# Norms by two products with ones, an inverse root and a Newton step, in a two-layer encoder trunk on one core

## The chip, the cores and the metric

The kernel runs on one core of a Trainium2 chip. The time is device microseconds of one execution, the median over runs. The engines are PE (TensorE, with its weight loads PEld), DVE (VectorE), ACT (ScalarE), POOL (GpSimd) and SP (SyncE, which only issues DMAs here). Each engine works through its own queue in order.

## The reference, cut to what matters

`x` is 512 x 1024. Layer 0 has an mLSTM token mixer, layer 1 a band attention over keys and values that both come from the output of layer 0; each layer ends in a gated MLP, the channel mixer. What the change touches is the RMSNorm ahead of three of these blocks:

```python
def rmsnorm(x, g):
    x32 = x.astype(jnp.float32)
    y = x32 * lax.rsqrt(jnp.mean(x32 * x32, axis=-1, keepdims=True) + EPS)
    return (y * g.astype(jnp.float32)).astype(x.dtype)

# layer 0: x = x + concat(mLSTM, memory attention) @ w_out
x = x + conv_ffn(rmsnorm(x, norm_ffn_g[0]), ...)          # place 1
k, v = split(rmsnorm(x, kv_norm_g) @ w_kv)                # place 2
# layer 1: h = rmsnorm(x, norm_mix_g[1]), the same factor as place 2
x = x + concat(band attention, memory attention) @ w_out
x = x + conv_ffn(rmsnorm(x, norm_ffn_g[1]), ...)          # place 3
```

The fourth norm (ahead of layer 0) and the last one are done by other code and stay.

## The kernel before

Activations are kept transposed: `xT[j]` is a tile of 128 features by 512 tokens, eight tiles for the 1024 features. Every matrix product is done in three passes over a high and a low part (`mm3`, lines 158 to 160: high x high, high x low, low x high), each a 128x512 matmul. High parts are casts on ACT (line 114), low parts subtractions on DVE (line 115). A *unit* is one such group of three; a projection `project` of 1024 features onto 128 columns has eight units, and a weight tile goes through a raw buffer (`wr`, loaded by SP at line 127), a high and a low one (`wh`, `wl`), three of each. A cast into `wh` therefore waits for the last product that reads the buffer three projections back.

For three tiles of each channel mixer (`up` of tiles 1, 2 and 3) the low part is made without DVE: `summed_weights` casts the high part on ACT (line 147), writes its negative on ACT into a `pt` buffer (line 148), and POOL issues a DMA that reads the weights once more and adds them there (line 149).

A norm's factor depends on the token, so it is a row of 512 values that is wanted on all 128 partitions. The class `Norm` does this. While the tiles of `x` are finished, `add` sums their squares into `acc` (a tile of 128 x 512, a buffer of the tag `rb`), and `scaled` makes the high and low parts of the tiles times the gain, without the factor; the products run on these, and their results are multiplied by `row` afterwards. `finish` turns `acc` into `row`. It is a generator woven into the units of the projections that follow: `yield 5.4` lets 5 units of the filler be issued, and the rest is carried on to the next yield. In the three places the filler is: the first `gate` and `up` projections of channel mixer 0 (place 1) and of channel mixer 1 (place 3), 16 units; and the first value and key projections of layer 1 (place 2). A `row` used by `plain` multiplies the products of `gate` (line 670), by `forms` the tiles of `x` (line 685), and by `project_pair` the values and keys (line 1293), where PE then transposes the values (line 1304).

The same row by two products with ones, an inverse root on ACT and a Newton step on DVE stands already in the mLSTM heads (lines 1197 to 1202), for another norm.

In the three places the framework's scheduler sets the order of the work that the program issues, and then each engine keeps it.

Of the kernel before, what the change touches and what calls it, by code (L numbers as in the profile page):

```python
# [9 lines left out]
F32 = mybir.dt.float32  # L10
F32R = mybir.dt.float32r
I32 = mybir.dt.int32
AF = mybir.ActivationFunctionType
ALU = mybir.AluOpType
AX = mybir.AxisListType

P = 128
D = 1024
S = 512
KT = D // P  # L20
TT = S // P
# [9 lines left out]
EPS = 1e-6  # L31
# [16 lines left out]
def f(ap):  # L48
    return ap.bitcast(F32)
# [3 lines left out]
def trunk(  # L53
# [18 lines left out]
    nc = tc.nc  # L72
    V, A, G = nc.vector, nc.scalar, nc.gpsimd

    cpool = ctx.enter_context(tc.tile_pool(name="cpool", bufs=1))
# [8 lines left out]
    def sb(tag, shape, dtype=F32):  # L84
        count[0] += 1
        return pool.tile(shape, dtype, tag=tag, name=f"{tag}{count[0]}", bufs=bufs[tag])

    def ps(tag):
        count[0] += 1
        return psum.tile([P, S], F32, tag=tag, name=f"p{tag}{count[0]}", bufs=pbufs[tag])  # L90

    def small(n=4):
# [5 lines left out]
    ones = cpool.tile([P, P], F32, name="ones")  # L98
    V.memset(ones, 1.0)
    onesr = cpool.tile([P, P], F32R, name="onesr")  # L100
# [5 lines left out]
        out=maskf, in_=maskf, pattern=[[1, P]], base=0, channel_multiplier=-1,  # L106
        compare_op=ALU.is_ge, fill=NEG,
    )
    HEADS = (slice(0, HD), slice(HD, P))

    pin = tc.keep_in_program_order
# [125 lines left out]
    class Norm:  # L237
# [14 lines left out]
        def finish(self):  # L252

            yield 5.4
            o = ps("sc")
            for T in range(TT):
                tc.keep_in_program_order(
                    nc.tensor.matmul(
                        o[:, T : T + 1], self.acc[:, T * P : (T + 1) * P], ones[:, 0:1], start=True, stop=True
                    )  # L260
                )
            self.factor(o[:, :TT])
            yield 8.4
            self.spread()

        def factor(self, o):
            self.scale(o)
            self.diagonals()

        def scale(self, o):  # L270
            v = small()
# [133 lines left out]
    with tc.manual_schedule(engines={mybir.EngineType.PE, mybir.EngineType.Activation, mybir.EngineType.DVE}):  # L405
# [9 lines left out]
        for q in range(KT // 2 + 1):  # L415
            if q < KT // 2:
# [6 lines left out]
                hi, lo = sb("u", [P, S], F32R), sb("u", [P, S], F32R)  # L423
# [50 lines left out]
    def head_queries(t, scale=1.0):  # L474
        qs, ls = ([sb("u", [P, S], F32R) for _ in range(2)] for _ in range(2))
        for h, r in enumerate(HEADS):
            G.memset(f(ls[h])[HEADS[1 - h], :], 0.0)
            A.activation(qs[h][r, :], t[r, :], AF.Copy, scale=scale)
            V.scalar_tensor_tensor(ls[h][r, :], t[r, :], scale, f(qs[h])[r, :], op0=ALU.mult, op1=ALU.subtract)
        for h, r in enumerate(HEADS):  # L480
            A.copy(qs[h][HEADS[1 - h], :], f(qs[h])[r, :])
        return qs, ls

    def head_keys(t):
        ks = [sb("u", [P, S], F32R) for _ in range(2)]
        for h, r in enumerate(HEADS):
            A.copy(ks[h][r, :], t[r, :])
            V.tensor_tensor(out=ks[h][HEADS[1 - h], :], in0=t[r, :], in1=f(ks[h])[r, :], op=ALU.subtract)
        return ks
# [774 lines left out]
    for j in range(KT):  # L1264
        wh, wl = weights(rows(ffn_w_down[0], j * P, P, FT - LAST, FT), LAST, P)
        o = ps("mm")
# [252 lines left out]
```

## Time and profile before

| | |
|---|---|
| median of 3 runs | 1203.21 us (1202.51 to 1204.61) |
| profiled execution | 1202.59 us, its span 1200.6 us |
| granted PE clock | 0.998 |
| busy: PE, PEld, DVE, ACT, POOL | 99%, 87%, 78%, 60%, 12% of the span |
| norm at place 1, 2, 3: column sums on PE | at 278.4, 627.4, 843.6 us |

Times in the profile count from the start of the span. A row of a timeline gives start, duration (both us), engine, line, operation, tile written and tiles read (buffer numbers left out), shapes, count, and in brackets the idle time of that engine just before and what ended it. `SPq` and `POOLq` rows are issues of DMAs. A PE row's duration is modelled and overlaps with the next one; the distance from row to row is what a matmul costs.

### The profile page before, as it was taken

What the parts mean: (1) busy time and instruction counts of PE and PEld (TensorE: products, weight loads), DVE (VectorE), ACT (ScalarE), POOL (GpSimd) and SP (SyncE); (2) the same over time, 40 slices, a digit from 0 to 9 for tenths busy, and PEclk for the clock granted to TensorE, in tenths of its full rate; (3) what the DMA queues carried; (4) which work ended last, traced back from release to release, by engine and by line L of the source; (5) the groups of instructions that cost most, each with busy time, mean ns of one, the idle gap of its engine ahead of it and who ended that gap; (6) DMA issues with size and microseconds to landing.
All of it is one profiled execution on the core that took longest, in us unless ns stands there. A gap on an engine that the chain in (4) does not pass through costs nothing.

```text
span 1200.6 us, 18610 instructions
## 1 busy us (share of the span) xinstructions
PE 1182.9 (99%) x6963; PEld 1046.7 (87%) x6963; DVE 940.4 (78%) x1670; ACT 723.3 (60%) x1270; POOL 146.9 (12%) x234
## 2 busy tenths in 40 slices
PE   9999999999999999999999999999999999999997
PEld 8988888878899999999888888888789999999986
DVE  6877797787968777777698888997896877777755
ACT  4547797655656555555566677775565655555545
POOL 0203201011021111111020000101101011011100
PEclk9999999999999999999999999999999999999999
DMA  8636422448466677665563313244836465666551
GB/s 278 202 106 155 102 73 71 145 137 190 102 139 171 157 163 163 158 145 117 142 212 112 88 59 96 73 139 152 185 86 143 120 142 135 141 141 138 118 158 70
DMA packets 208747, 162.83 MB, mean 136 GB/s; under 512 B 8484, under 2 KB 188170, under 8 KB 208658
## 3 DMA queue, kind: packets, MB, share of 16 engines
q1 hardware_dynamic: 186450, 120.78, 34.5%
q0 software_dynamic: 22208, 40.87, 18.1%
q8 instruction: 54, 0.88, 0.3%
q14 instruction: 35, 0.29, 0.1%
HBM read 133.09 MB, written 32.47 MB: 138 GB/s over the span
## 4 chain that ended last, share of the span: by engine, by line
PE 78%; issue 12%; DVE 3%; DMA 3%; ACT 2%; POOL 1%; SPq 0%; POOLq 0%; ACTq 0%; DVEq 0%
PE pmm L158 15%; PE pmm L159 15%; PE pmm L160 15%; PE ptr L159 5%; PE ptr L158 5%; PE ptr L160 5%; PE psc L160 5%; PE psc L159 5%; PE psc L158 5%; DMA pt<-in_ffn_w_up_dram 2%; PE psc L497 1%; PE ptr L1346 1%; POOL xspill L611 1%; PE ptr L1367 0%; PE ptr L1368 0%
## 5 line engine op out<-in xcount | busy, mean ns | idle before, releaser
L158 PE MATMUL pmm<-u,wh 128*128 128x512 f32 (+1 forms) x968 | 335.6, 347 | 2.2 <-ACT u L114 2.1
L159 PE MATMUL pmm<-u,wh 128*128 128x512 f32 (+1 forms) x968 | 333.4, 345 | 0.0
L160 PE MATMUL pmm<-u,wl 128*128 128x512 f32 (+1 forms) x968 | 333.2, 345 | 0.0
L115 DVE TENSOR_TENSOR wl<-wr,wh 128x1024 fp32r<-128x1024 f32 (+4 forms) x172 | 195.2, 1136 | 110.0 <-ACT wh L114 108.9
L114 ACT CAST wh<-wr 128x1024 fp32r<-128x1024 f32 (+4 forms) x172 | 168.6, 981 | 98.0 <-PE pmm L159 43.1
L158 PEld LDWEIGHTS pmm<-u,wh 128*128 128x128 f32 x968 | 183.6, 190 | 21.1 <-ACT u L114 3.1
L160 PEld LDWEIGHTS pmm<-u,wl 128*128 128x128 f32 x968 | 183.6, 190 | 20.9
L159 PEld LDWEIGHTS pmm<-u,wh 128*128 128x128 f32 x968 | 183.8, 190 | 18.6 <-DVE u L115 0.6
L159 PE MATMUL ptr<-u,wh 128*128 128x512 f32 x272 | 106.5, 392 | 0.0
L158 PE MATMUL ptr<-u,wh 128*128 128x512 f32 x272 | 106.4, 392 | 0.0
L160 PE MATMUL ptr<-u,wl 128*128 128x512 f32 x272 | 105.8, 389 | 0.0
L733 POOL DMA_DIRECT2D xspill<-t x64 | 56.1, 877 | 401.0 <-ACT t L732 391.4
L160 PE MATMUL pmm<-u,u 128*128 128x256 f32 x296 | 84.0, 284 | 0.2 <-DVE u L115 0.2
L158 PE MATMUL pmm<-u,u 128*128 128x256 f32 x296 | 84.0, 284 | 0.0
L159 PE MATMUL pmm<-u,u 128*128 128x256 f32 x296 | 83.8, 283 | 0.0
L158 PE MATMUL psc<-u,wh 128*128 128x256 f32 (+1 forms) x232 | 76.1, 328 | 0.0
L159 PE MATMUL psc<-u,wh 128*128 128x256 f32 (+1 forms) x232 | 75.9, 327 | 0.0
L732 ACT COPY t<-ptr 128x512 f32<-128x512 f32 x64 | 37.4, 585 | 62.2 <-PE ptr L160 62.2
L115 DVE TENSOR_TENSOR u<-pt,u 128x512 fp32r<-128x512 f32 x102 | 69.8, 688 | 6.2 <-ACT u L114 3.0
L114 ACT CAST u<-pt 128x512 fp32r<-128x512 f32 x102 | 63.0, 617 | 11.4 <-DVE pt L848 11.3
L911 ACT ACTIVATE t<-t 128x512 f32<-128x512 f32 x34 | 21.6, 634 | 79.4 <-DVE t L637 79.4
L115 DVE TENSOR_TENSOR u<-t,u 128x512 fp32r<-128x512 f32 x78 | 53.4, 688 | 20.3 <-ACT u L114 19.8
(281 smaller groups left out, 2559.2 us busy)
## 6 DMA issues: line engine op xcount, KB each, us to landing
wr<-in_ffn_w_up_dram SPq DMA_DIRECT2D x54, 512.0 KB, 4.8
pt<-in_ffn_w_up_dram SPq DMA_DIRECT2D x34, 512.0 KB, 6.5
wr<-in_ffn_w_down_dram SPq DMA_DIRECT2D x34, 512.0 KB, 3.8
xspill<-t POOLq DMA_DIRECT2D x64, 256.0 KB, 4.8
wr<-in_a_w_in_dram SPq DMA_DIRECT2D x20, 512.0 KB, 3.9
xspill<-u POOLq DMA_DIRECT2D x32, 256.0 KB, 2.9
u<-xspill SPq DMA_DIRECT2D x32, 256.0 KB, 5.1
wr<-in_w_kv_dram SPq DMA_DIRECT2D x12, 512.0 KB, 4.1
```

The lines of the kernel that those rows point to most:

```text
L114: high = A.copy(hi, src) if on_act else V.tensor_copy(hi, src)
L115: low = V.tensor_tensor(out=lo, in0=src, in1=f(hi), op=ALU.subtract)
L158: nc.tensor.matmul(o, lh, rh, start=first, stop=False, skip_group_check=more)
L159: nc.tensor.matmul(o, lh, rl, start=False, stop=False, skip_group_check=more)
L160: nc.tensor.matmul(o, ll, rh, start=False, stop=last, skip_group_check=more)
L497: nc.tensor.matmul(o, a, b, start=first and i == 0, stop=i == 1)
L611: pin(G.dma_start(xspill[j], xT[j]))
L732: A.copy(t, o)
L733: G.dma_start(xspill[j], t, accum_op=ALU.add)
L911: A.activation(self.acc, self.acc, AF.Silu)
L1346: nc.tensor.transpose(tp[:, b * P : (b + 1) * P], es[T, h][:, b * P : (b + 1) * P], ident)
```

## The change

`finish` is rewritten and `factor` goes. Before: after 5 units, four matmuls with one column of ones sum `acc` over the partitions for 128 tokens each (tokens on partitions); then on DVE a shift-and-multiply start and three Newton steps on 128 x 4 values, a split into high and low, and two diagonal matrices of 128 x 512; after 13 units two products with ones spread these over all partitions, and a copy makes `row`. Now: after 5 units `acc` plus a constant is split into `hi` (ACT) and `lo` (DVE); after 8 units two products with ones sum and spread in one; ACT takes the inverse root, and DVE does one Newton step on 128 x 512. The constant is `epsc`, a new 128 x 1 tile.

```diff
+    epsc = cpool.tile([P, 1], F32, name="epsc")
+    V.memset(epsc, EPS * D / P)
...
         def finish(self):
 
             yield 5.4
+            hi, lo = sb("t", [P, S], F32R), sb("t", [P, S], F32R)
+            A.activation(hi, self.acc, AF.Identity, bias=epsc)
+            V.scalar_tensor_tensor(lo, self.acc, epsc, f(hi), op0=ALU.add, op1=ALU.subtract)
+            yield 2.6
             o = ps("sc")
-            for T in range(TT):
-                tc.keep_in_program_order(
-                    nc.tensor.matmul(
-                        o[:, T : T + 1], self.acc[:, T * P : (T + 1) * P], ones[:, 0:1], start=True, stop=True
-                    )
-                )
-            self.factor(o[:, :TT])
-            yield 8.4
-            self.spread()
-
-        def factor(self, o):
-            self.scale(o)
-            self.diagonals()
+            for i, part in enumerate((hi, lo)):
+                nc.tensor.matmul(o, onesr, part, start=i == 0, stop=i == 1)
+            self.row, t = sb("rb", [P, S]), sb("t", [P, S])
+            A.activation(self.row, o, AF.Abs_reciprocal_sqrt, scale=1.0 / D)
+            V.tensor_mul(t, self.row, self.row)
+            V.scalar_tensor_tensor(t, t, -0.5 / D, o, op0=ALU.mult, op1=ALU.mult)
+            V.scalar_tensor_tensor(self.row, t, 1.5, self.row, op0=ALU.add, op1=ALU.mult)
```

The lines below the new tile are three further down in the changed kernel, and those below `finish` one further (line 148 is 151 there, line 644 is 645).

PE's queue at place 1 before, from the fifth unit of `gate` (`pmm`) on; the column sums stand between the fifth and the sixth:

```order
L158 MATMUL pmm_2884<-u_2753,wh_2880 128x512
L159 MATMUL pmm_2884<-u_2754,wh_2880 128x512
L160 MATMUL pmm_2884<-u_2753,wl_2881 128x512
L258 MATMUL psc_2900<-ones,rb_2715 128x1 x4
L158 MATMUL pmm_2884<-u_2793,wh_2880 128x512
```

And in the changed kernel, from the eighth unit of `gate` to the first of `up` (`psc_2930`):

```order
L161 MATMUL pmm_2886<-u_2875,wh_2882 128x512
L162 MATMUL pmm_2886<-u_2876,wh_2882 128x512
L163 MATMUL pmm_2886<-u_2875,wl_2883 128x512
L264 MATMUL psc_2915<-t_2902,onesr 128x512
L264 MATMUL psc_2915<-t_2903,onesr 128x512
L161 MATMUL psc_2930<-u_2719,wh_2926 128x512
```

The column sums are gone, and the pair with ones, which stood after the fifth unit of `up`, now stands between `gate` and `up`.

ACT's queue at place 3 before, from the last tile of `x` (squares and gain) on:

```order
L249 ACTIVATE t_9053<-u_8449 128x512
L286 ACTIVATE u_9056<-u_8449,cols_519 128x512
L147 CAST wh_9224<-wr_9222 128x1024
L148 ACTIVATE pt_9064<-wh_9224 128x1024
L644 ACTIVATE t_9160<-t_9161,cols_771 128x512
```

And in the changed kernel:

```order
L252 ACTIVATE t_9015<-u_8411 128x512
L287 ACTIVATE u_9018<-u_8411,cols_521 128x512
L259 ACTIVATE t_9049<-rb_8860,epsc 128x512
L150 CAST wh_9166<-wr_9164 128x1024
L266 ACT_TABLE_LOAD
L266 ACTIVATE rb_9065<-psc_9062 128x512
L151 ACTIVATE pt_9026<-wh_9166 128x1024
L645 ACTIVATE t_9102<-t_9103,cols_773 128x512
```

`hi` (L259) stands ahead of the cast of the high part of `up`, tile 1; a table load and the inverse root (L266) stand between that cast and the write of its negative (L151). At place 1 the order is the same without the table load; at place 2 there is a load too, and a plain weight cast stands ahead of it. Over the whole program ACT has two table loads more.

## The prediction

> **What bounds the kernel now.** I read the page first, then the waits of the matmul engine (PE), then the timelines of all engines around the three norms, and last the shares of the DMA queues there. The page's engine table, and the second longest wait of PE (engine, line, what it waited for: total us, times, longest; the longest, 2.1 us, stands ahead of the first norm):
>
> ```profile
> PE 1182.9 (99%) x6963; PEld 1046.7 (87%) x6963; DVE 940.4 (78%) x1670; ACT 723.3 (60%) x1270; POOL 146.9 (12%) x234
> PE psc L160 <- DMA pt<-in_ffn_w_up_dram: 1.7, 2, 1.1
> ```
>
> PE is busy all the time and hardly waits, so PE time removed is time won, unless PE then waits longer. That one is the only wait near the norms: the third product of project `up` of tile 1 needs the low weight part that POOL accumulates by DMA (L149). Place 1 is the first mixer's norm, place 2 the norm ahead of token mixer B, place 3 the second mixer's norm. PE at place 1 (start, us, line, operation, and idle time before it in brackets):
>
> ```profile
> 270.02 0.39 PE L160 MATMUL pmm<-u,wl 128*128 128x512 f32 x1
> ...
> 278.18 0.39 PE L160 MATMUL pmm<-u,wl 128*128 128x512 f32 x1
> 278.41 0.95 PE L258 MATMUL psc<-ones,rb 128*128 128x1 f32 x8
> ...
> 281.39 0.39 PE L158 MATMUL psc<-u,wh 128*128 128x512 f32 x1
> ...
> 293.99 0.50 PE L160 MATMUL psc<-u,pt 128*128 128x512 f32 x1 [0.61 <-DMA pt<-in_ffn_w_up_dram]
> ```
>
> **The change, part by part.** *The column sums (L258) go.* Between the first two rows lie 36 steps: (278.18 - 270.02)/36 = 0.227 us each. From the L258 row to the 281.39 row lie nine products, 9 x 0.227 = 2.04 us, but 2.98 passed: the four small matmuls cost 0.94 us. The same at the other two places, nine products after the L258 row:
>
> ```profile
> 627.40 0.95 PE L258 MATMUL psc<-ones,rb 128*128 128x1 f32 x8
> 630.39 0.39 PE L158 MATMUL pmm<-u,wh 128*128 128x512 f32 x1
> 843.62 0.95 PE L258 MATMUL psc<-ones,rb 128*128 128x1 f32 x8
> 846.61 0.39 PE L158 MATMUL psc<-u,wh 128*128 128x512 f32 x1
> ```
>
> 2.99 - 2.04 = 0.95 at both. I take 0.94 three times: 2.82 us off PE. The pair of products with ones (L234) has the same shapes as before and is only moved, from after 13 units to after 8; zero.
>
> *Inputs of the pair.* It now needs `hi` (ACT) and `lo` (DVE) of the sum of squares. DVE at place 1:
>
> ```profile
> 277.25 0.69 DVE L250 TENSOR_TENSOR rb<-rb,t 128x512 f32<-128x512 f32 x1
> 277.85 0.75 DVE L287 SCALAR_TENSOR_TENSOR u<-u,cols,u 128x512 fp32r<-128x512 f32 x1
> 279.39 0.16 DVE L272 TENSOR_SCALAR s<-psc 128x4 f32<-128x4 f32 x1 [0.79 <-PE psc L258]
> 282.06 1.29 DVE L221 TENSOR_TENSOR t<-ident,s 128x512 fp32r<-128x512 f32 x2
> 285.46 0.69 DVE L282 COPY rb<-psc 128x512 f32<-128x512 f32 x1 [2.12 <-PE psc L234]
> 290.76 1.22 DVE L115 TENSOR_TENSOR wl<-wr,wh 128x1024 fp32r<-128x1024 f32 x1
> ```
>
> The sum is ready at 277.94. ACT is idle then (its next row is 281.40, below): `hi` by about 278.75, at the 0.6 to 0.8 us of ACT's 128x512 operations. `lo`, like L287, 0.75 us behind it, by 279.4. PE reaches the pair at 278.41 + 9 x 0.227 = 280.45. Cover 1.0 us, so no wait; if it were gone, each 0.1 us of it would cost PE 0.1. DVE loses the run 279.39 to 283.35 and the copy, 4.6 us, and gets `lo` and three Newton steps, 0.75 + 3 x 0.69 = 2.8; DVE does not bound, zero.
>
> *ACT and the DMA behind it.* This decides. ACT gets `hi`, the inverse root, and at places 2 and 3 one more table load, 3 x 1.3 + 2 x 1.3 = 6.5 us of an engine that is 60% busy. But it is an ordered queue, and the inverse root now stands between L147 and L148, whose result POOL's accumulating DMA waits for, and `up` of tile 1 behind that. ACT, SP and POOL at places 1 and 3, and PE's wait at place 3:
>
> ```profile
> 281.40 1.05 ACT L147 CAST wh<-wr 128x1024 fp32r<-128x1024 f32 x1 [4.18 <-issue]
> 282.49 1.06 ACT L148 ACTIVATE pt<-wh 128x1024 fp32r<-128x1024 f32 x1
> 283.85 1.62 POOL L149 DMA_DIRECT2D pt<-in_ffn_w_up_dram  x1 [7.12 <-ACT pt L148]
> 292.01 0.37 SPq L127 DMA_DIRECT2D wr<-in_ffn_w_up_dram  x1
> 846.62 1.05 ACT L147 CAST wh<-wr 128x1024 fp32r<-128x1024 f32 x1 [4.18 <-issue]
> 847.70 0.37 SPq L127 DMA_DIRECT2D wr<-in_ffn_w_up_dram  x1
> 847.70 1.06 ACT L148 ACTIVATE pt<-wh 128x1024 fp32r<-128x1024 f32 x1
> 848.12 1.67 SPq L743 DMA_DIRECT2D pt<-in_ffn_w_up_dram  x2
> 849.06 1.63 POOL L149 DMA_DIRECT2D pt<-in_ffn_w_up_dram  x1 [7.12 <-ACT pt L148]
> 859.69 0.50 PE L160 MATMUL psc<-u,pt 128*128 128x512 f32 x1 [1.10 <-DMA pt<-in_ffn_w_up_dram]
> ```
>
> L147 starts as gate 0's products end (281.39 above) and free its buffer, so it moves 0.94 us forward with PE. The price of the inverse root and its load is that of the same formula in the mLSTM heads:
>
> ```profile
> 129.23 0.62 ACT L114 CAST t<-t 128x512 fp32r<-128x512 f32 x1 [2.48 <-DVE t L1189]
> 129.87 1.28 ACT L1199 ACT_TABLE_LOAD   x1
> 129.91 0.50 PE L1197 MATMUL psc<-t,onesr 128*128 128x512 f32 x1 [0.24 <-ACT t L114]
> 131.17 0.60 ACT L1199 ACTIVATE t<-psc 128x512 f32<-128x512 f32 x1
> ```
>
> The load starts where the cast ends and does not wait for PE. So at place 1 (no load): L147 at 280.46, root at 281.54, L148 at 282.14 instead of 282.49, POOL's issue 0.35 us earlier at 283.50. At place 3: L147 at 845.68, load 846.76, root 848.06, L148 848.66 instead of 847.70; POOL's issue 0.96 us later, at 850.02, while PE comes 0.94 us earlier. Does the landing follow that issue? The queue shares at place 3 (q1 is SP's queue, q0 POOL's: packets, MB, share of 16 engines), for the microseconds from 853, from 854 and from 858:
>
> ```profile
> q1 hardware_dynamic: 499, 0.26, 95.6%
> ...
> q0 software_dynamic: 208, 0.11, 86.4%
> q1 hardware_dynamic: 268, 0.13, 46.5%
> ...
> q1 hardware_dynamic: 218, 0.11, 40.4%
> q0 software_dynamic: 32, 0.02, 15.8%
> ```
>
> POOL issued at 849.06, yet in 853 it has no row, so it moves nothing, and in 854 it starts, as SP's three transfers (3 x 0.5 MB, issued 847.70 to 849.79) run out. So the landing hangs on SP's transfers, which wait for L147 and come 0.94 us earlier with PE. I take that for the sum: both waits, 0.61 and 1.10, stay, and the whole 0.94 is won at each place. What hides POOL's later issue is SP's 1.5 MB: the issue ends at 850.02 + 1.63 = 851.65, the earliest moment of those packets moves to 854.0 - 0.94 = 853.1, cover 1.4 us; beyond it each us costs one. The other end of the price, the landing following the issue, is 0.59 us at place 1 and 1.90 at place 3; the packets are nearer to the first.
>
> [...]
>
> *Place 2.* `row` is needed by the transposes of the values:
>
> ```profile
> 630.40 1.05 ACT L114 CAST wh<-wr 128x1024 fp32r<-128x1024 f32 x1 [3.57 <-issue]
> 635.17 0.69 DVE L1293 TENSOR_TENSOR t<-pmm,rb 128x512 f32<-128x512 f32 x1
> 636.32 0.60 PE L1304 MATMUL pmm<-ident,t 128*128 128x128 f32 x4
> ```
>
> The cast also follows PE (the wh buffer that the finished projection frees) and comes at 629.46; load and root end at 629.46 + 1.08 + 1.30 + 0.60 = 632.44; three DVE steps of 0.72 give `row` at 634.6, L1293 ends at 635.3; PE wants it at 636.32 - 0.94 = 635.38. Cover 0.1 us. This chains six steps whose rows are each good to some 0.05 us, so 0 to 0.3 us may be lost; I take zero.
>
> *What comes late next.* At place 1 `row` is ready 2 us earlier than before (root ends 282.14, plus 2.2: 284.3, instead of 286.15), so the split at 290.76 and SP's next load behind it (292.01) come up to 2 us earlier, 1.1 more than PE, and meet the tail of POOL's accumulation. The price lies between 0 and 0.5 us: at place 3, where SP's load already meets that tail (859.69 waits while 858 shows both queues), the wait is 1.10 against 0.61 at place 1. I take 0.2.
>
> Sum: 3 x 0.94 - 0.2 = 2.6 us. The profiled execution took 1202.59 (span 1200.6); the median of the runs is 1203.21, so 1200.6 by the median, 1200.0 by the profiled one. No change can be told within 0.2%, 2.4 us: 1200.8 to 1205.6.
>
> **The rivals.** *The landing follows POOL's issue.* Place 1 then wins 0.35, place 2 0.94, and place 3 loses 0.96: 0.33 us won, 1202.9. For it: the accumulation is on the path at both places. Against it: the packets above.
>
> *Slower: SP's next load overtakes the accumulation's tail.* It moves 0.52 MB, 2.0 us at the 0.26 MB a us of the row. If the tail stood still for that, each mixer would lose 2.0 us against 0.94 won; place 2 still wins 0.94: 2 x 2.0 - 2.82 = 1.2 us slower, 1204.4. It decides where that load starts ahead of POOL's last packet and the loss in each mixer is beyond 1.41 us. For it: in 858 the tail is down to 32 packets a us while SP's load starts. Against it: both still move there, and only at place 1 does the load come nearer.
>
> *Row late at place 2.* Cover is 0.1 us there, and all beyond it is PE idle. If the switch of tables held the root back by once more a load, 1.28 us, 1.2 us would be lost: 1201.8. For it: the cover is thin. Against it: the root followed its load at once in the mLSTM rows (1.30 us from start to start, 1.28 of it the load). [...]
>
> *The waits go too.* If the accumulation lost its queueing behind the 1.5 MB, up to 0.61 + 1.10 more would be won: 1198.9. No row speaks for it.
>
> **How the numbers follow.** The forecast (2.82 less 0 to 0.8: 1200.4 to 1201.2) has 0.62, the landing by issue 0.16, the overtaken tail 0.09, the late row 0.06, the waits gone 0.07. The range leaves out the two outer cases, 0.16 together, and takes in 1202.9 and 1200.4 with 0.5 to 1 us for the scatter of the runs (1202.51 to 1204.61 before): 1199.3 to 1203.4. Faster by over 0.2% (below 1200.8): 0.7 of the forecast, 0.43, and the last case, 0.07, 0.50. Slower by over 0.2% (above 1205.6) is beyond every case, 0.04 for what I do not see. The rest, 0.46, is no change.
>
> **What would show it.** PE's rows at the pair: no L258, no idle, steps of 0.227. POOL's issue at place 3 about 1 us later against L147, and PE's wait for `pt` still near 0.6 and 1.1; if that wait is near 3 us, the landing follows the issue. At place 2 no idle before the transposes. Wrong would be: a wait for `hi`, or waits for `pt` at tiles 2 and 3.

## The result and the profile after

The changed kernel takes 1198.72 us, the median of six runs (1198.22 to 1199.65), against 1203.20 for the kernel before beside it (1202.51 to 1204.61): ratio 0.9963, 95% interval 0.9950 to 0.9976. That is 4.5 us faster, and 0.6 us below the predicted range. Its profiled execution took 1198.67 us, span 1196.9 us, against 1202.59 and 1200.6 before.

The engine table of the page after:

```profile
PE 1181.6 (99%) x6939; PEld 1046.2 (87%) x6939; DVE 935.5 (78%) x1632; ACT 729.1 (61%) x1278; POOL 145.5 (12%) x234
```

24 PE rows are gone, eight for each norm, as predicted. Of the waits of PE over the whole program, the three longest after, the start's load, and the same load before:

```profile
PE pmm L161 <- ACT u L117: 2.1, 1, 2.1
PE psc L1198 <- ACT t L117: 1.5, 4, 0.4
PE pmm L161 <- ACT wh L117: 1.4, 1, 1.4
...
PE psc L421 <- DMA u<-in_mem_dram: 0.5, 1, 0.5
```

```profile
PE psc L420 <- DMA u<-in_mem_dram: 1.1, 1, 1.1
```

The line for `pt`, 1.7 us over two waits before, has no counterpart. PE at place 1, from the fifth unit of `gate` to the first product that reads `pt`:

```profile
279.29 0.39 PE L163 MATMUL pmm<-u,wl 128*128 128x512 f32 x1
...
281.57 0.62 PE L264 MATMUL psc<-t,onesr 128*128 128x512 f32 x2
282.03 0.40 PE L161 MATMUL psc<-u,wh 128*128 128x512 f32 x1
...
293.16 0.39 PE L162 MATMUL psc<-u,wh 128*128 128x512 f32 x1
293.48 0.50 PE L163 MATMUL psc<-u,pt 128*128 128x512 f32 x1
```

And at places 2 and 3, again from the fifth unit on:

```profile
626.66 0.39 PE L163 MATMUL pmm<-u,wl 128*128 128x512 f32 x1
...
628.93 0.63 PE L264 MATMUL psc<-t,onesr 128*128 128x512 f32 x2
...
634.86 0.66 PE L1305 MATMUL pmm<-ident,t 128*128 128x128 f32 x4
...
841.97 0.39 PE L163 MATMUL pmm<-u,wl 128*128 128x512 f32 x1
...
844.25 0.63 PE L264 MATMUL psc<-t,onesr 128*128 128x512 f32 x2
...
855.84 0.39 PE L162 MATMUL psc<-u,wh 128*128 128x512 f32 x1
856.06 0.39 PE L163 MATMUL psc<-u,pt 128*128 128x512 f32 x1
```

Before, the fifth units ended with these rows at places 2 and 3, and these rows stood just ahead of the product that waited at places 1 and 3 (293.99 and 859.69):

```profile
627.17 0.39 PE L160 MATMUL pmm<-u,wl 128*128 128x512 f32 x1
...
843.40 0.39 PE L160 MATMUL pmm<-u,wl 128*128 128x512 f32 x1
```

```profile
292.99 0.39 PE L159 MATMUL psc<-u,wh 128*128 128x512 f32 x1
...
858.20 0.39 PE L159 MATMUL psc<-u,wh 128*128 128x512 f32 x1
```

From the fifth unit to the same later row, before less after:

- place 1: (293.99 - 278.18) - (293.48 - 279.29) = 15.81 - 14.19 = 1.62 us;
- place 2: (636.32 - 627.17) - (634.86 - 626.66) = 9.15 - 8.20 = 0.95 us;
- place 3: (859.69 - 843.40) - (856.06 - 841.97) = 16.29 - 14.09 = 2.20 us.

The column sums are 0.94 of each. The rest, 0.7 and 1.3, is the wait for `pt`. Counted from row to row, less a step of 0.227, the product came 0.77 us late before and 0.09 after at place 1 (1.00 and 0.32 from the row ahead), and 1.26 before and 0 after at place 3 (1.49 and 0.22). The idle time in the brackets, 0.61 and 1.10, is 0.16 less, since a row's modelled 0.39 us reach beyond the step. The three places make 4.8 us, and the medians 4.5. The spans of the profiled pair differ by 3.7 only, because the profiled execution after has a loss at 250 us that the one before has not, far from the norms. There PE stands 2.11 us behind ACT in both kernels; the rows of 250 to 260 us, before and then after (after the span come busy us of PE, PEld, DVE, ACT and POOL, the granted PE clock, DMA share, GB/s):

```profile
250.00:260.00 10.00, 8.54 (x36) 6.78 (x37) 7.20 (x11) 5.40 (x10) 1.63 (x3) 1.00 0.51 166
```

```profile
250.00:260.00 10.00, 8.70 (x31) 7.11 (x32) 6.08 (x9) 4.14 (x9) 1.63 (x3) 0.83 0.42 136
```

The clock was granted at 0.83 and PE got through five products fewer, 5 x 0.227 = 1.1 us. The start, where the load's wait is 0.6 shorter, gives part of it back. A second profile of the changed kernel (after_again, below) has no wait for `pt` either, and the same 0.83 behind the hole.

ACT, SP and POOL at place 3 after:

```profile
844.25 1.05 ACT L150 CAST wh<-wr 128x1024 fp32r<-128x1024 f32 x1 [1.76 <-PE pmm L162]
845.32 1.28 ACT L266 ACT_TABLE_LOAD   x1
845.75 1.61 SPq L744 DMA_DIRECT2D pt<-in_ffn_w_up_dram  x2
846.61 0.60 ACT L266 ACTIVATE rb<-psc 128x512 f32<-128x512 f32 x1
847.11 1.05 ACT L151 ACTIVATE pt<-wh 128x1024 fp32r<-128x1024 f32 x1
848.46 1.63 POOL L152 DMA_DIRECT2D pt<-in_ffn_w_up_dram  x1 [7.94 <-ACT pt L151]
```

POOL's issue comes 4.21 us behind the cast of `wh` (2.44 before), nearly as late as the 4.34 of the prediction. And still no wait. So a late issue by itself does not make the wait. The shares of the DMA queues hold a third queue, q8, whose kind the page gives as instruction. In both pages it has 54 packets, one about every 22 us, and from one of them to the next PE and PEld together have 253 rows on average before and 254 after (181 to 314), so I read its packets as fetches of PE's instructions:

```profile
q8 instruction: 54, 0.88, 0.3%
```

The quarter microseconds in which such a packet starts near the accumulation (before from 291.50 and from 856.75; after from 295.00 and from 857.75):

```profile
q0 software_dynamic: 85, 0.04, 138.1%
q8 instruction: 1, 0.02, 23.7%
...
q0 software_dynamic: 89, 0.05, 143.6%
q8 instruction: 1, 0.02, 23.5%
```

```profile
q1 hardware_dynamic: 48, 0.05, 88.5%
q8 instruction: 1, 0.02, 23.0%
...
q1 hardware_dynamic: 165, 0.08, 111.7%
q8 instruction: 1, 0.02, 25.7%
```

One packet of 16 KB takes 23.7% of 16 engines over 0.25 us, 0.95 us of engine time, where the 85 packets beside it take 138.1%, 0.065 us each. That one of the sixteen is away for nearly 1 us is my estimate from these two numbers; no trace names the engine of a packet. Before, the packet falls into the accumulation both times (q0's row beside it), and in its last part; after, only SP's queue is beside it, the accumulation having landed. What POOL's queue moves at its end, place 3, before in half microseconds from 857.5:

```profile
q0 software_dynamic: 29, 0.01, 26.2%
...
q0 software_dynamic: 21, 0.01, 22.7%
...
q0 software_dynamic: 11, 0.01, 9.0%
```

and after from 854.5:

```profile
q0 software_dynamic: 128, 0.06, 98.1%
...
q0 software_dynamic: 13, 0.00, 7.9%
```

After, the queue goes from 128 packets to none within 1 us; before, it drips for 1.5 us behind the fetch, a few packets at a time.

### The profile page after: what moved, and what is told of

The parts are those of the page before. It is cut to its first block, busy times and chain, and to the rows that moved or that the text cites. A ratio compares the mean times of both kernels' runs of the same rounds, so it can differ in the third digit from the quotient of the medians.

```text
span 1196.9 us, 18533 instructions
## 1 busy us (share of the span) xinstructions
PE 1181.6 (99%) x6939; PEld 1046.2 (87%) x6939; DVE 935.5 (78%) x1632; ACT 729.1 (61%) x1278; POOL 145.5 (12%) x234
## 4 chain that ended last, share of the span: by engine, by line
PE 94%; DVE 3%; ACT 2%; issue 0%; DMA 0%; SPq 0%; ACTq 0%; DVEq 0%
PE pmm L161 18%; PE pmm L163 18%; PE pmm L162 18%; PE ptr L161 6%; PE ptr L162 6%; PE ptr L163 6%; PE psc L163 5%; PE psc L162 5%; PE psc L161 5%; PE psc L498 2%; PE ptr L1347 1%; PE ptr L581 1%; PE ptr L1368 1%; PE ptr L1369 1%; PE ptr L567 1%; ACT wh L117 0%
```

## The experiments

Two theories. *Fetch*: an instruction fetch of PE that falls into the accumulation makes it land late; the change takes 24 matmul rows of PE away, with their weight loads, so the fetches fall elsewhere. *Order*: in the kernel before, POOL's issue stands amid SP's issues, and after it behind them, and that lets the accumulation land earlier. In the table below C is the start of the cast of `wh` that precedes the write of the negative; the third to fifth columns belong to place 1, the others to place 3. All are us, the fetch to within 0.25, and the wait is PE's idle time for `pt` as the trace has it. A kernel ran beside one of five sets of runs of the kernel before, each set on one chip, so its median is to be set against that one: 1203.20 for after; 1202.07 for sums_kept, before_late2, before_few_warm and after_filled; 1202.90 for after_late2, after_late3, few_warm_late2 and after_more_warm; 1202.83 for after_again, after_filled_again, place2_only and places13; 1202.92 for the rest.

| kernel | median | POOL - C | fetch - C | wait | POOL - C | fetch - C | wait |
|---|---|---|---|---|---|---|---|
| before | 1203.20 | 2.45 | 10.1 | 0.61 | 2.44 | 10.1 | 1.10 |
| after | 1198.72 | 2.80 | 13.4 | 0 | 4.21 | 13.5 | 0 |
| after_again | 1198.32 | 2.79 | 12.8 | 0 | 4.21 | 13.2 | 0 |
| sums_kept | 1203.10 | 2.79 | 10.3 | 0.63 | 4.21 | 7.8 | 0.37 |
| before_late2 | 1201.77 | 4.63 | 10.2 | 0.57 | 4.64 | 7.4 | 0.67 |
| before_few_warm | 1202.74 | 2.45 | 13.6 | 0.23 | 2.45 | 14.9 | 0.64 |
| few_warm_again | | 2.45 | 13.7 | 0 | 2.44 | 13.4 | 0.20 |
| few_warm_late2 | 1203.26 | 4.63 | 13.9 | 0.26 | 4.63 | 13.8 | 0 |
| few_warm_late2_again | | 4.63 | 14.1 | 0 | 4.62 | 13.8 | 0 |
| after_filled | 1197.79 | 2.80 | 9.9 | 0.57 | 4.2 | 14 | 0 |
| after_filled_again | 1198.37 | 2.8 | 10.3 | 0.58 | 4.2 | 14.3 | 0 |
| after_more_warm | 1202.91 | 2.8 | 9.8 | 0.31 | 4.2 | 10.8 | 0 |
| place2_only | 1202.11 | 2.45 | 9.8 | 0.22 | 2.44 | 10.6 | 1.09 |
| places13 | 1199.35 | 2.8 | 13.0 | 0 | 4.2 | 14.8 | 0 |
| after_late2 | 1199.81 | 4.98 | 12.7 | 0 | 6.39 | 15.8 | 1.06 |
| after_late3 | 1202.72 | 6.63 | 15.2 | 1.16 | 8.04 | 16.9 | 2.52 |
| pair_later | 1198.77 | 2.45 | 13.9 | 0 | 2.44 | 12.9 | 0 |
| pair_later_again | | 2.45 | 14.6 | 0.19 | 2.45 | 13.2 | 0.18 |

**The column sums back in.** The changed kernel with the four matmuls kept, their result unused:

```diff
+            for T in range(TT):
+                tc.keep_in_program_order(
+                    nc.tensor.matmul(
+                        o[:, T : T + 1], self.acc[:, T * P : (T + 1) * P], ones[:, 0:1], start=True, stop=True
+                    )
+                )
             yield 2.6
```

> The changed kernel with the four column-sum matmuls put back after the fifth unit of each norm, their result unused. Only PE's queue gets longer again, by 0.94 us and 16 PE instructions at each place; ACT, POOL and SP keep the changed order. Theory A (fetch): before the change one 16 KB instruction fetch of PE (queue q8) fell into POOL's accumulation at places 1 and 3 and held up one DMA engine; the change removes 16 PE instructions at place 1 and 48 up to place 3, which moves the fetch later, past the landing. With the instructions back the fetch is back near 2 us before the landing at place 1, and PE waits about 0.6 us at place 1 and 1.1 us at place 3 again: 2.8 + 1.7 us over the changed kernel, near 1203. Theory B (order of issue): the waits went because POOL now issues after SP's loads instead of between them. Then the waits stay below 0.2 us and the time is 2.8 us over the changed kernel, near 1201.5.

Measured: 1203.10 us (1201.28 to 1203.78), against 1202.07 for the kernel before beside it; ratio 1.0006, 0.9996 to 1.0015. All of the gain is gone, not only the 2.8 us of the sums: the waits are back with them, at place 1 and at place 3:

```profile
295.37 0.50 PE L163 MATMUL psc<-u,pt 128*128 128x512 f32 x1 [0.63 <-DMA pt<-in_ffn_w_up_dram]
...
860.55 0.50 PE L163 MATMUL psc<-u,pt 128*128 128x512 f32 x1 [0.37 <-DMA pt<-in_ffn_w_up_dram]
```

So the waits come with the four matmuls and go without them, while the new work of ACT is there in both kernels. Its waits are 0.7 us shorter than before's, and yet it is not faster; in its profile the clock from 250 to 260 us was granted at 0.83, as in that of after, which may be part of it.

**POOL's issue later in the kernel before.** The write of the negative done three times for tile 1:

```diff
-        A.activation(lo, f(hi), AF.Copy, scale=-1.0)
+        for _ in range(1 + late):
+            A.activation(lo, f(hi), AF.Copy, scale=-1.0)
```

> The kernel before, with the write of the negative high part of tile 1 (line 148) done three times in a row, so that POOL issues its accumulation some 2.0 us later at places 1 and 3, after SP's loads; PE's instructions are those of before. Theory A (fetch): the waits stay at about 0.6 and 1.1 us, and the time within 0.3 us of before. Theory B (order of issue): the waits go to below 0.2 us as in the changed kernel, 1.6 us faster than before. The rival of the prediction, landing follows POOL's issue: the waits grow by 2 us each, 4 us slower.

Measured: 1201.77 us, ratio 0.9999, 0.9990 to 1.0009. POOL's issue 2.2 us later costs nothing: the wait at place 1 is 0.57 against 0.61, at place 3 0.67 against 1.10. The landing does not follow the issue. At place 3 the fetch moved too, so that place tells nothing between the theories.

**Fewer instructions in the kernel before.** PE runs nine small warming matmuls at the start; eight are left out, and nothing else is touched:

```diff
-        warm(6)
+        warm(1)
...
-                warm(3)
+                pass
```

> The kernel before with eight of the nine warming matmuls at the start left out, which are 32 PE instructions, so that each later instruction fetch of PE comes about 16 matmuls, 3.6 us, later in the program. Nothing else is changed at the norms. Theory A (fetch): the fetch that fell at 291.5 and 856.8 comes near 295 and 860, after the landings, and PE's waits at places 1 and 3 go below 0.3 us, 1.5 us won there (the start may lose a us or two with a colder PE). Theory B: the waits stay at 0.6 and 1.1.

> The kernel before with fewer warming matmuls at the start once more, for a second profile. The first had the fetch 14.9 us after the cast at place 3, outside the accumulation, and a wait for pt of 0.64 us. Theory of the order: about 0.6 again. Theory of the fetch alone: under 0.3, and the 0.64 was chance.

Measured: 1202.74 us (ratio 1.0001, 0.9991 to 1.0010); the single run 1201.96. The fetch moves from 10.1 us behind the cast to 13.4 to 14.9, and the waits, 1.71 together before, are 0.87 in the one profile and 0.20 in the other. So the norm needn't be touched for them to shrink. The time does not show it, since the cast at place 1 comes 2.0 and 0.9 us later than before: the start, with fewer warming matmuls, takes it back. The 0.64 at place 3 in the first profile, which spoke for the order, did not come again:

```profile
860.75 0.50 PE L160 MATMUL psc<-u,pt 128*128 128x512 f32 x1 [0.64 <-DMA pt<-in_ffn_w_up_dram]
```

```profile
859.24 0.50 PE L160 MATMUL psc<-u,pt 128*128 128x512 f32 x1 [0.20 <-DMA pt<-in_ffn_w_up_dram]
```

The same with the write three times over, so that the issue alone differs and the fetch stays outside:

> The kernel before with few warming matmuls and with POOL's issue 2.1 us later. With few warming matmuls alone the fetch was past the landing at both places; the wait at place 1 was 0.2 us, but at place 3 0.6 us stayed, with one DMA engine lagging. If that rest comes from the order of POOL's issue and SP's loads, it goes here too (below 0.2 us). If it is scatter of the DMA engines, or another cause, it stays anywhere between 0 and 0.7.

> The kernel before with fewer warming matmuls and the write of the negative three times over for tile 1, once more, for a second profile; its POOL issue comes 4.6 us after the cast, behind SP's loads. The first had no wait for pt at place 3. Theory of the order: 0 to 0.2 again, unless a fetch falls 7 to 12 us after the cast. Theory of the fetch alone: no difference to the same kernel without the repeated writes.

Measured: 1203.26 us (ratio 1.0004, 0.9993 to 1.0016); 1201.88 in the single run. No wait at place 3 in both, against 0.64 and 0.20 with the early issue. With the fetch out of the way, the order of the issues still counts for something there. At place 1 it doesn't: 0.26 and 0 against 0.23 and 0.

**Instructions added to the changed kernel.** Eight products whose result nobody reads fill the PE hole at 250 us, and so count as instructions ahead of place 1:

```diff
-    run(chain(fill, outp.part(0, 4, 5), outp.part(1, 4, 5)))
+    run(fill)
+    spare = ps("sc")
+    for _ in range(8):
+        pin(nc.tensor.matmul(spare, onesr, mixes[0][0], start=True, stop=True))
+    run(chain(outp.part(0, 4, 5), outp.part(1, 4, 5)))
```

> The changed kernel with eight idle products with ones in the 2.1 us hole of PE ahead of the last units of the first output projection (near 249 us). In the profile of the changed kernel PE runs at half clock for some 2.5 us right behind that hole (granted clock 0.83 from 250 to 260), in that of before it does not. If the hole lets the clock fall, the filled kernel keeps 1.00 there, ends up to 1.2 us earlier than the changed one, about 1197.5 to 1198.7, and its mean clock is 0.998. The products are 32 instructions at most, so instruction fetches move earlier by 1.8 us, and at place 1 the fetch may come back to near 293: up to 0.3 us of wait there. Rival: the products delay the units behind them, up to 0.5 us slower.

> The changed kernel with the eight products in PE's hole, beside the changed one on the same chip. If the clock falls behind the hole in some runs and costs 1.25 us there, the filled kernel is 0.3 to 1.2 us faster than the changed one and scatters less. If not, the two agree within 0.3 us.

Measured: 1197.79 us (0.9965, 0.9952 to 0.9978) and 1198.37 (0.9963, 0.9949 to 0.9976). The fetch is back at 9.9 and 10.3 us behind the cast at place 1, and so is the wait:

```profile
292.11 0.50 PE L163 MATMUL psc<-u,pt 128*128 128x512 f32 x1 [0.57 <-DMA pt<-in_ffn_w_up_dram]
```

At place 3 the fetch stayed outside and there is no wait. The granted clock from 250 to 260 us was 1.00 here. What that wins goes in part at place 1 again; the median is no better than that of the changed kernel, 1198.32 beside the second one. Seven warming matmuls more at the start of the changed kernel, `warm(13)` for `warm(6)`:

> The changed kernel with seven warming matmuls more at the start, 28 PE instructions, so that PE's instruction fetches come earlier by some 14 matmuls or 3.2 us. At place 1 the fetch moves from 13.4 us behind the cast of line 150 to about 10, into the accumulation: theory A expects a wait near 0.6 us there again. At place 3 it moves from 13.5 to about 10 as well and gives 0.3 to 0.6 us. If the waits stay below 0.15 us with the fetch inside the accumulation, theory A falls.

Measured: 1202.91 us (1.0000, 0.9990 to 1.0011). The fetch comes at 9.8 with a wait of 0.31 at place 1, at 10.8 without one at place 3. Place 3 thus speaks against the theory of the fetch by the expectation's own test: a fetch inside the accumulation does not always make PE wait. Most of the 4 us lost is not in these waits; the profiled execution, the fastest of its eight, has span 1198.3 and shows only part of it, and where the rest goes is not shown.

**How far the issue may slip.** The write done three and four times in the changed kernel:

> The changed kernel with the write of the negative high part of tile 1 (line 151) done three times, so that POOL issues its accumulation another 2.1 us later at places 1 and 3. If the landing hangs on SP's loads (the prediction's step), it does not move as long as POOL's first packet can still come before SP's loads run out: the shortest time from POOL's issue to its first packet is 2.3 us where no load is ahead. At place 1: 284.4 + 2.1 + 2.3 = 288.8, where the packets start at 288.9 anyway: no wait. At place 3: 848.5 + 2.1 + 2.3 = 852.9 against 851.4: 1.5 us later, with a slack of some 0.7 us a wait of 0.8 us. Sum 0.8 us slower than the changed kernel. If the landing follows POOL's issue: about 1.5 to 2 us of wait at each, 3.5 us slower.

> The same with four writes; the scheduler puts the fourth behind the next tap (line 645), so POOL's issue comes 3.8 us later than in the changed kernel. By the cover of the prediction: first packets 1.7 us later at place 1 and 3.4 us later at place 3, waits of about 1.5 and 2.7 us, 4 us slower than the changed kernel, about as slow as before. If the landing follows POOL's issue from the start: 3.5 us at each, 7 us slower.

Measured: 1199.81 us (0.9977, 0.9965 to 0.9989) and 1202.72 (1.0007, 0.9998 to 1.0017), with waits of 0 and 1.06, and of 1.16 and 2.52. At place 3 the issue 2.18 and 3.83 us later costs 1.06 and 2.52: a cover of 1.1 to 1.3 us, where the prediction had 1.4, and beyond it each us of delay costs about one. The packets show why. In all eighteen profiles the accumulation's first packet comes 7.2 to 7.7 us behind the cast wherever POOL's issue stands at 2.4 to 5.0, and 2.33 us after the issue in the three cases where that is later (place 3 of after_late2, both places of after_late3).

**The early issue in the changed kernel.** The pair with ones three units later at places 1 and 3, so that the root stands behind the write of the negative. The instructions of every engine are the same, but SP's next weight load moves too: it is issued 12.19 us behind the cast at place 3, against 11.06 in the changed kernel and 10.60 in the one before.

```diff
-                weave(self.norm.finish(), both, 1)
+                weave(self.norm.finish(5.6), both, 1)      # yield 5.6 in place of yield 2.6
```

> The changed kernel with the pair of products with ones three units later (after 11 units instead of 8) at places 1 and 3, so that the root stands behind the write of the negative (L151) on ACT and POOL issues its DMA about 2.4 us after the start of the cast L150, amid SP's loads, as in the kernel before. The PE instructions are as many as in the changed kernel. Theory of the order (POOL's issue amid SP's loads makes the accumulation land later at place 3, whatever the instruction fetch does): PE waits 0.6 to 1.1 us for pt at place 3, at least 0.4 if no fetch falls between 7 and 12 us after the cast; time 0.6 to 1 us above the changed kernel, 1199.0 to 1199.8. Theory of the fetch alone: where the fetch comes more than 12 us after the cast, both waits stay under 0.3 and the time is that of the changed kernel, 1198.2 to 1198.8.

> The same kernel once more, for a second profile. Theory of the order: a wait for pt of 0.4 to 1.1 us at place 3 again. Theory of the fetch alone: a wait only if the fetch falls 7 to 12 us after the cast there.

Measured: 1198.77 us (0.9966, 0.9951 to 0.9980); 1200.40 in the single run. POOL's issue is back amid SP's, 2.44 us behind the cast, and PE does not wait:

```profile
843.64 1.05 ACT L150 CAST wh<-wr 128x1024 fp32r<-128x1024 f32 x1 [1.77 <-PE pmm L162]
...
846.08 1.63 POOL L152 DMA_DIRECT2D pt<-in_ffn_w_up_dram  x1 [6.18 <-ACT pt L151]
...
855.45 0.45 PE L163 MATMUL psc<-u,pt 128*128 128x512 f32 x1
```

In the second profile it waits 0.18. An early issue alone does not make a wait of 1.10, then; the theory of the order falls as its whole cause.

**The change at some places only**, and whole once more. The old norm kept at places 1 and 3, then at place 2 alone:

```diff
-                weave(self.norm.finish(), both, 1)
+                weave(self.norm.finish_before(), both, 1)
```

```diff
-    weave(norm.finish(), fill, 1)
+    weave(norm.finish_before(), fill, 1)
```

> The new norm at place 2 alone; places 1 and 3 as before. PE loses the column sums once: 0.92 us. No accumulation hangs on place 2, so theory A and theory B both expect the wait at place 1 to stay near 0.6 us; at place 3 the fetch comes 16 PE instructions later (about 12 us behind the cast of line 147 instead of 10.1), at the edge of the landing, so a wait of 0.6 to 1.1 us. Time 0.9 to 1.4 us faster than before. If `row` came late at place 2 (the prediction's rival), PE would idle ahead of the transposes and less would be won.

> The new norm at places 1 and 3, the old one at place 2. PE loses the column sums twice, 1.84 us. Theory A: the fetch is past the landing at place 1 as in the changed kernel (wait below 0.2 us); at place 3, 32 PE instructions later than before, at 13 to 14 us behind the cast, too (wait near 0). So 1.84 + 0.5 to 1.6 us faster than before, 2.3 to 3.5 us.

> The changed kernel once more, beside the kernel before on the same chip, since the runs of before have spread over 3 us in the later comparisons (median 1202.4 of 53). The trace gave 0.92 us of PE at each of three places and 2.0 us of waits, 4.8 in all, of which up to 1.25 can be lost to a slower clock behind the 2.1 us hole of PE. If all of that is steady: 4.5 us faster, ratio near 0.9963. If the waits of before vary from run to run, so that only the PE part is steady: nearer to 3.3 us, 0.9973.

Measured, beside a kernel before of 1202.83: place 2 alone 1202.11 (0.9993, 0.9984 to 1.0002), places 1 and 3 alone 1199.35 (0.9971, 0.9960 to 0.9981), all three 1198.32 (0.9963, 0.9950 to 0.9975). That is 0.7, 3.5 and 4.5 us. Place 2, which has no accumulation, is worth its column sums, 0.94, within the scatter; the two others are worth 1.9 of column sums and 1.6 of waits. One expectation missed: the wait of place2_only at place 1 was 0.22 and not near 0.6, although up to there its PE does what it does in the kernel before and the fetch stands inside. One profile's wait can be off by 0.4.

**Taken together.** At place 1, a fetch 9.8 to 10.3 us behind the cast goes with a wait of 0.22 to 0.63 in seven profiles, mean 0.50; one 12.7 us or more behind it with 0 to 0.26 in ten, mean 0.07 (after_late3 left out, whose issue is itself late). At place 3 with the early issue the means are 1.10 of two inside and 0.26 of four outside; with the issue at 4.2 to 4.6 us, 0.35 of three inside and 0 of seven outside.

The traces also have the time of each update of the accumulation's semaphore, sixteen for this transfer. At place 1 the fifteenth comes 11.61 us behind the cast on average in the seven profiles with the fetch inside (11.29 before), and 11.60 in the ten others (11.59 after). The last comes at 12.43 and 11.81 (12.54 before, 11.87 after). So one update of sixteen is late, and the rest are not. That the fetch holds up one engine is my reading of this; it was not shown. A late sixteenth can have another cause too: at place 3 of before_few_warm it came 0.87 us behind the fifteenth with the fetch far off, and there SP's loads ran on until 10.7 us behind the cast, a packet every 0.08 us. With POOL's issue at 2.8 us or later they were through by 8.7 in every profile.

So at place 1 the fetch is the cause: before_few_warm moves it out with the issue where it was, and the waits fall; before_late2 moves the issue with the fetch inside, and the wait stays. At place 3 the fetch and the early issue both count, and the change removed both. The two means inside, 1.10 and 0.35, and the two outside, 0.26 and 0, give the fetch 0.35 to 0.84 of the 1.10 and the order 0.26 to 0.75; no run here splits them better.

Open: why a fetch inside costs PE nothing in one profile (after_more_warm at place 3) and 0.67 in another (few profiles, and the fetches stand elsewhere, 7.4 to 10.8). And where a fetch falls cannot be counted out: it moves by some 3.4 us at place 1 where eight products come or go, though these are 1.8 us of PE, and at place 3 by no more, though there 24 rows are gone, and after_filled leaves it there outside. The rows from one fetch to the next, 181 to 314 before and after, are not even.

## Why the prediction was wrong

- *The column sums cost 0.94 each*: right. The stretch at place 2, where nothing else changed, shortened by 0.95.
- *The pair moved at zero, `hi` and `lo` in time*: right. From the fifth unit's last row to the pair are 281.57 - 279.29 = 2.28 us for ten steps, no idle.
- *ACT's queue*: right at place 3, where POOL's issue came 4.21 us behind the cast for a predicted 4.34. At place 1 it was 2.80 for 3.04, since the root followed its cast at 0.96 us.
- *The landing hangs on SP's transfers, not on POOL's issue; cover 1.4 us*: right, with 1.1 to 1.3. The 1.4 counted from the end of the issue, 1.63 us after its start; the first packets came 2.33 us after the start in the three late cases, and 2.25 to 2.29 at tiles 2 and 3 before and after. The rival "the landing follows POOL's issue" falls with before_late2, where an issue 2.2 us later made no wait longer (0.57 and 0.67 us against 0.61 and 1.10), and with the place 3 of after.
- *"I take that for the sum: both waits, 0.61 and 1.10, stay"*: wrong, and this is the step that failed. It read each wait as the time of SP's and POOL's bytes, which nothing in the change shortens. By the means above some 0.4 us of the first hung on a fetch of PE's instructions in the accumulation's last part, and of the second 0.35 to 0.84 on such a fetch and the rest on POOL's early issue; the change moved the one out and the other back. The step had only q0 and q1 of those windows; q8 stood in the page as 0.3% of the DMA engines, a share over the whole program, and I passed over it. The sum with both waits gone: 2.82 + 0.61 + 1.10 = 4.53, and 4.48 was measured. That the two agree so closely is in part luck, as a single profile's wait scatters by some 0.4 us.
- *"The waits go too", 1198.9, "No row speaks for it", 0.07*: that case came, with 1198.72. A row did speak for it, the one of q8 at 291.50 and at 856.75, and at place 1 it was not through less queueing behind the 1.5 MB, as the rival had it. Whether the change would move the fetch out rather than in could not be read from the trace; that it stood at a place from which a change of PE's instructions could move it could. The case deserved some 0.3, and the range should have reached 1198.
- *What comes late next, 0.2*: the load came nearer as forecast, and cost nothing that shows. At place 1 it was issued at 291.21, 9.64 us behind the cast (10.61 before). It met the accumulation's tail, here from 292.5 to 293.0, and PE's product was 0.09 us late there, against 0.77 before:

```profile
q1 hardware_dynamic: 195, 0.10, 73.1%
q0 software_dynamic: 36, 0.02, 26.0%
```

No wait for `pt` stands at tiles 2 and 3. The rival in which that load overtakes the tail falls.

- *Place 2, cover 0.1, taken as zero*: right, with a cover of 0.06. Its steps came some 0.5 us earlier than forecast, and so did PE's transposes, at 634.86 for 635.38. ACT and DVE there after:

```profile
630.00 1.28 ACT L266 ACT_TABLE_LOAD   x1
631.30 0.60 ACT L266 ACTIVATE rb<-psc 128x512 f32<-128x512 f32 x1
...
634.11 0.69 DVE L1294 TENSOR_TENSOR t<-pmm,rb 128x512 f32<-128x512 f32 x1
```

Load to root is 1.30 us, as in the mLSTM rows. L1293 (L1294 now) ends at 634.80, and PE's transposes follow at 634.86, right behind their unit.

## What to carry to other kernels

Before a DMA wait on the critical path is taken as fixed, look at every queue in the last microseconds of that transfer, the instruction queue too; a share of 0.3% over the program says nothing of one packet in the wrong microsecond. Where an edit adds or removes instructions of the busiest engine ahead of a tight landing, its fetches can move (here from 10.1 to 13.4 us behind the cast at place 1), and the range has to hold both outcomes, wait there and wait gone. Test such a cause by changing the instruction count alone, at a place far from the wait, and take a second profile before a 0.5 us wait in one is believed. Where two causes went with one change, say which share each can have; here the order of the issues, set aside as beaten, still held part of the wait at place 3.

## What the runs showed of the hardware

One packet of 16 KB of q8, read here as a fetch of PE's instructions, took 0.95 us (before, from 291.50), against 0.065 us for each packet of the accumulation beside it. In the seven profiles where such a packet fell into the accumulation at place 1, the last of the sixteen updates came 0.6 us later than in the ten others (12.43 against 11.81 us behind the cast), the fifteenth no later (11.61 and 11.60), and PE waited 0.4 us longer (0.50 against 0.07).

The hole of 2.11 us in PE's work, which ends at 251.46 us before and at 251.30 after, was followed by a granted clock of 1.00 from 250 to 260 us before and of 0.83 after (also in the profiles of after_again and sums_kept); the kernel that fills the hole, after_filled, has 1.00 in both of its profiles. In the trace of after the clock stood at half for 3.41 us, from 251.21 to 254.63, where the expectation of after_filled has some 2.5; in that of before it stayed at full. So the same hole came with either clock, and what decides between them was not shown.
